# Attention on one core: the value products, transposes and sums of a group gathered in one place of TensorE's order

## The chip, the cores and the metric

The kernel runs on one core of a Trainium2 chip. The metric is the device time of one execution in microseconds; the kernel before took 2106.49 us (median of three runs, 2105.7 to 2106.67).

## What is computed

One layer of an encoder on 1024 tokens of 1024 features, all in float32: attention, a layer norm with a scaled residual, a mixture of experts (4 of 32 for each token), and a second layer norm. The change is in the attention alone:

```python
def attention_mixer(x, w_qkv, q_norm, k_norm, w_o):
    q, k, v = jnp.split(x @ w_qkv, ...)        # 16 heads of q, 4 of k and v, 64 features each
    q, k = apply_rope(rms_norm(q, q_norm)), apply_rope(rms_norm(k, k_norm))
    s = jnp.einsum('bqkgd,bskd->bkgqs', q_blk, k) * scale     # blocks of 128 queries
    p = jax.nn.softmax(s, axis=-1)
    o = jnp.einsum('bkgqs,bskd->bqkgd', p, v)
    return o.reshape(bsz, seq, N_Q_HEADS * HEAD_DIM) @ w_o
```

Every head of k and v serves four heads of q.

## The kernel before, in words

The kernel has four stages: the projections to q, k and v with their norms and rotary positions (to about 160 us of the profile), attention (to about 530 us), the output projection with the norm and the routing, and the experts, whose weights are streamed from memory. A float32 product that must be exact is made of parts that were rounded and what the rounding left ("hi" and "lo").

Attention goes over 8 tiles of 128 queries, `i`, and in each over the 4 heads of keys, `g`. One pair is a *group*, `n = 4 i + g`, with four heads of queries; there are `NG = 32` of them. In a group the loop goes over 8 tiles of 128 keys, `k`; one turn of it is called a step here.

- `probs(n, k)` (L439): two matmuls of 512 columns make the scores of one tile of keys (tile `st`, two buffers), with the negated maxima already in them; ScalarE's exponential writes `pt` (L447, twelve buffers). GpSimd adds up `pt` over the tiles of keys into `acc`, and VectorE makes the last addition (L451).
- `scores(n + 2, m, hf)` (L427): the scores of the group after next the other way round, two matmuls into a tile `sc` of 1024 columns (two buffers), and VectorE's maximum over it (`nm`, L437), four of them a group.
- `maxima_a`, `maxima_b` (L143, L149): the maxima in two parts, transposed by TensorE (`tpm`), and spread by VectorE into the operand `q2` (L155), of which ScalarE copies the other half (L152).
- `pv(n, k)` (L454): the value products of two tiles of keys, side by side on the two halves of TensorE's columns, summed in `po` (one buffer). Each of them shows as two records in the trace. `close_a(n)` (L462) adds the two halves (ScalarE's copy `ob`, L469, and VectorE's two additions, L472).
- `scale_a(i)`, `scale_b(i, hf)` (L478, L494): once a tile of queries, the sums of the exponentials over the keys (`su`, 16 matmuls, 32 records), their reciprocals by a chain on VectorE (L486 to L491), and two matmuls `rb` that spread them, with a multiplication of half the outputs behind each (L499). Then the outputs go to memory.
- `stack_q(i + 1, h)` (L158): four transposes of queries of the next tile (`tpq`), which ScalarE and VectorE take apart (L168 to L172). `tpm`, `tpq`, `su` and `rb` share one buffer in PSUM.

What sets the order: the framework's scheduler places each engine's instructions by their order in the program, when their operands are expected, and by what room is free. Where the code opens `manual_schedule` for an engine, that engine's instructions are kept as they are written. Before, TensorE had an order by hand in the first group alone (L534 to L567). In the others the scheduler placed `pv` pair by pair between the scores, near the places where the loop calls it (steps 3, 5 and 7, and step 1 of the next group for the last pair). VectorE, ScalarE and GpSimd are placed by the scheduler in both kernels. Every engine works through its queue in the order that it was given.

Of the kernel before, what the change touches and what calls it, by code (L numbers as in the profile page):

```python
# [42 lines left out]
def trunk_kernel(ctx: ExitStack, tc: tile.TileContext, x, w_qkv, q_norm, k_norm, w_o,  # L43
# [59 lines left out]
    # ones on the rows that meet the maxima  # L103
# [3 lines left out]
    # the heads' high parts again, and below them the maxima, each at its own head  # L107
    q2s = [p_kv.tile([P, 4, P], F32R, name="q2_0")]
    nc.gpsimd.memset(q2s[0][HD:P].bitcast(F32), 0.0)
    # sums of the heads (g, a, j) on rows (g, r, a, j): r = 0 gives its high part and r = 1 its low part  # L110
# [20 lines left out]
    def first_scores(s, ps):  # L131
        # the first four heads' maxima, in halves
        hf, m = divmod(s, 4)
        if s == 0:
            nms[0] = p_xq.tile([P, 4], F32, tag="nm", bufs=3, name="nm0")
            nms["h"] = p_xq.tile([P, 4, 2], F32, name="nmh")
        sc = ps.tile([P, 512], F32, tag="qkv2", name=f"sc0_{s}")
        mm(sc, qs[0][:, m, :], kT_hi[:, 0, hf * 512:(hf + 1) * 512])
        nc.vector.tensor_reduce(nms["h"][:, m, hf:hf + 1], sc, AX.X, ALU.max, negate=True)
        if s == 7:  # L140
            nc.vector.tensor_reduce(nms[0], nms.pop("h"), AX.X, ALU.min)
# [16 lines left out]
    def stack_q(i, h, ps):  # L158
        # eight heads: the upper half of the partitions holds what rounding leaves
        if h == 0:  # L160
            qs[i] = p_xq.tile([P, NH, P], F32R, tag="cols", bufs=2, name=f"qs{i}")
        qv = qs[i][:, 8 * h:8 * h + 8, :].rearrange("p (j a) t -> p j a t", a=2)
        tp = ps.tile([P, 4, P], F32, tag="tp", name=f"tpq{i}_{h}")
        for c in range(4):
            j = 4 * h + c
            nc.tensor.transpose(tp[:, c, :], ql[i][:, j * P:(j + 1) * P], ident)
        odd = p_xq.tile([P, 4, P], F32R, tag="odd", name=f"odd{i}_{h}")
        nc.scalar.copy(qv[0:HD, :, 0, :], tp[0:HD])  # L168
        nc.scalar.copy(odd[HD:P], tp[HD:P])
        nc.vector.tensor_tensor(qv[HD:P, :, 0, :], tp[0:HD], qv[0:HD, :, 0, :].bitcast(F32), ALU.subtract)  # L170
        nc.vector.tensor_tensor(qv[HD:P, :, 1, :], tp[HD:P], odd[HD:P].bitcast(F32), ALU.subtract)
        nc.scalar.copy(qv[0:HD, :, 1, :], odd[HD:P].bitcast(F32))  # L172

# [1 line left out]
    QKV = (NH + 2 * NKV) * HD  # L175
    nqk = NH + NKV
    with tc.tile_pool(name="p1", bufs=1, side="right", reuse_waits="tile") as p1, \
# [68 lines left out]
        # cosines and sines with the norms' weights and the scale in them  # L246
# [123 lines left out]
    # pieces of the experts' weights, in the order in which they are used  # L370
# [12 lines left out]
    def fetch(upto):  # L383
        while nxt[0] < min(upto, len(seq)):
            e, kind, n = seq[nxt[0]]
            # the first table entry is awaited early, so that the first gathers go ahead of what follows
            e2 = max(e, 2)
            if (e > 1 or nxt[0] == 12) and e2 not in ev:
                with tc.issue_after(last[0]):
                    ev[e2] = nc.values_load(eid[0:1, e2:e2 + 1], engines=[mybir.EngineType.SP],  # L390
                                           min_val=0, max_val=NE - 1)
            x_ = ds(ev[e], 1) if e > 1 else slice(e, e + 1)
            w = slot(order[nxt[0] % len(order)], f"w{e}{kind}{n}")
            with ExitStack() as es:
                if last[0] is not None:
                    es.enter_context(tc.issue_after(last[0]))
                if kind == "g":
                    got = nc.sync.dma_start(w, w_gu[x_, n * P:(n + 1) * P, :].rearrange("o p n -> p (o n)"))
                else:
                    got = nc.sync.dma_start(  # L400
                        w.rearrange("p (k n) -> p k n", k=2),
                        w_dn[x_, 2 * n * P:2 * (n + 1) * P, :].rearrange("o (k p) n -> p (o k) n", p=P))
            last[0] = got.ins
            raw[nxt[0]] = w
            nxt[0] += 1

    # rows of four KB that the output projection and then the experts use
# [12 lines left out]
    with tc.tile_pool(name="p2", bufs=1, side="right", reuse_waits="tile") as p2, \  # L420
# [6 lines left out]
        def scores(n, m, hf):  # L427
            # queries on the partitions, for the maxima
            i, g = divmod(n, NKV)
            if hf == 0:  # L430
                sc[n, m] = ps_s.tile([P, T], F32, tag="sc", name=f"sc{n}_{m}")
            sl = slice(hf * 512, (hf + 1) * 512)
            mm(sc[n, m][:, sl], qs[i][:, 4 * g + m, :], kT_hi[:, g, sl])
            if hf == 1:
                if m == 0:
                    nms[n] = p_xq.tile([P, 4], F32, tag="nm", bufs=3, name=f"nm{n}")
                nc.vector.tensor_reduce(nms[n][:, m:m + 1], sc.pop((n, m)), AX.X, ALU.max, negate=True)  # L437

        def probs(n, k):  # L439
            # keys on the partitions: scores less the maxima, then the exponentials  # L440
# [13 lines left out]
        def pv(n, k):  # L454
            # two tiles of keys side by side
            i, g = divmod(n, NKV)
            if k == 0:
                po[n] = ps_o.tile([P, 4 * P], F32, tag="po", name=f"po{n}")
            for b in range(2):
                mm(po[n][b * HD:(b + 1) * HD], vn[:, k + b, g, :], pts[n, k + b], k == 0, k == NT - 2)  # L460
# [17 lines left out]
        def scale_a(i):  # L478
            # one over the sums over the keys
# [36 lines left out]
        # the table of slots: rows without a token point past the tokens  # L516
# [12 lines left out]
        for r in (1, 2):  # L529
            q2s.append(p2.tile([P, 4, P], F32R, name=f"q2_{r}"))  # L530
            nc.gpsimd.memset(q2s[r][HD:P].bitcast(F32), 0.0)
        for n in range(NG + 1):
            i, g = divmod(n, NKV)
            if n == 0:  # L534
                first = ExitStack()
                first.enter_context(tc.manual_schedule(engines={mybir.EngineType.PE}))
            for k in range(NT):
# [9 lines left out]
                if k == (5 if n == 0 else 2) and n + 1 < NG:  # L547
                    maxima_b(n + 1, ps_t)
                if k == 1 and n > 0:
                    pv(n - 1, NT - 2)  # L550
                    close_a(n - 1)
                if g == 0 and n > 0:
                    if k == 4:
                        scale_a(i - 1)
                    elif k in (5, 7):
                        scale_b(i - 1, k // 7)
                if k in (3, 5, 7) and n < NG:
                    pv(n, k - 3)
                if n < NG and i + 1 < NT:
                    if g == 0 and k == 6:  # L560
                        load_q(i + 1)
                    if g in (1, 2) and k == 0:
                        stack_q(i + 1, g - 1, ps_t)
            if n + 2 < NG:
                maxima_a(n + 2)
            if n == 0:
                first.close()  # L567
            if i in (2, 3) and g == 2:
                load_o(i - 2)
            if i == 4 and g == 2:  # L570
                load_xr(0)
    es_kv.close()
    keep = ctx.enter_context(tc.tile_pool(name="keep", bufs=1, side="left", reuse_waits="tile"))

# [24 lines left out]
    # the first expert's place in the sequence is its own  # L599
# [31 lines left out]
    with tc.tile_pool(name="p3o", bufs=1, side="right", reuse_waits="tile") as p3o, \  # L631
# [43 lines left out]
        def norm_b(i):  # L675
# [7 lines left out]
            if i == NT - 1:  # L683
                # the table of the exponential comes while the engine waits
# [23 lines left out]
        def route_a2(i):  # L708
            x1T = x1Tn.pop(i)
            # a quarter of the features in each quarter of the columns  # L710
# [13 lines left out]
        def run(*gens):  # L724
            # in turn, an instruction of each
# [28 lines left out]
        def rows_of_first(i, mk, pp):  # L754
            # the slots of the first expert without a way through the table
# [67 lines left out]
        def f_gates(i):  # L823
            # the gates in two parts, twice over, as rows
# [22 lines left out]
        def f_add(i):  # L847
            # alpha * x1 plus the gated second biases of the experts
# [31 lines left out]
        def split_b(i):  # L880
            # the first biases as three parts of eight bits
# [54 lines left out]
        # rank (by count) of the expert at each position of the sequence  # L936
# [28 lines left out]
        # the last tile's way to the first expert's rows, with other work in its gaps  # L965
        L = NT - 1
        with tc.manual_schedule(engines={mybir.EngineType.DVE, mybir.EngineType.Activation,
# [39 lines left out]
            # experts in the order of their counts (the first two stay where they are)  # L1007
# [37 lines left out]
    with tc.tile_pool(name="moex", bufs=1, side="right", reuse_waits="tile") as mx, \  # L1045
# [7 lines left out]
        def slots(finish):  # L1053
            # slots of every expert: the first 128 rows, and the next 32 four times over (a quarter row each)
# [29 lines left out]
        def list_blocks():  # L1084
            # blocks of rows beyond what the unrolled experts take
# [78 lines left out]
        def turn_a(e, part):  # L1164
            if part == 0:
                # the last one has the room of a next expert's rows
# [43 lines left out]
        def gate_up(e, between):  # L1210
# [33 lines left out]
            if by_cols:  # L1244
                # the end goes column by column, and a half's activation as soon as it is there
# [101 lines left out]
    # the rows and the last norm's weights take slots of the stream  # L1347
# [141 lines left out]
```

## Time and profile before

| What | Value |
|---|---|
| time, median of three runs | 2106.49 us |
| span of the profiled execution | 2106.0 us |
| TensorE busy in the span | 2017.2 us (96%) |
| VectorE | 1631.0 us (77%) |
| ScalarE | 1286.0 us (61%) |
| GpSimd | 547.3 us (26%) |
| mean granted clock of TensorE | 0.984 |
| 500 MB moved, mean | 238 GB/s |

The table gives the busy time of each engine in the span; an engine can be busy while it isn't the one that the others wait for. The durations of matmuls overlap, since they are pipelined, so what one of them takes of TensorE's time is read from the distance of two starts. Where a row says "idle before", an arrow names what the engine waited for.

### The profile page before, as it was taken

How to read it: one execution, taken by the hardware profiler on the slowest of the kernel's cores; microseconds unless marked ns; L12 is line 12 of the kernel's file. 1: busy time of each engine (PE TensorE's matmuls, PEld its weight loads, DVE VectorE, ACT ScalarE, POOL GpSimd, SP SyncE). 2: the span in 40 equal slices, each digit the busy share in tenths (PEclk: the TensorE clock that was granted, in tenths of full speed). 3: DMA queues.
4: the chain of work that ended last, by engine and by line, in shares of the span. 5: the costliest groups of instructions: out<-in, count | busy, mean ns of one | idle time of the engine just before them, and what ended most of it. 6: DMA issues, size and time to landing. Idle time of an engine off the chain costs nothing. (4 is left out here: it accounts for less than half of the span.)

```text
span 2106.0 us, 27647 instructions
## 1 busy us (share of the span) xinstructions
PE 2017.2 (96%) x10091; PEld 1348.4 (64%) x10091; DVE 1631.0 (77%) x1771; ACT 1286.0 (61%) x1548; POOL 547.3 (26%) x382
## 2 busy tenths in 40 slices
PE   8999999999997999999999999999999999999990
PEld 6774444444675666666676776777767767677670
DVE  6658788877888777677787787877878778778786
ACT  5656556655555656566676666766756667667562
POOL 1216666675144201111211211111112111110004
PEclk9999999999998999999999999999999999999995
DMA  4116000000646777888888897998989988889765
GB/s 171 70 61 176 31 31 31 28 13 11 231 150 222 292 282 274 295 281 294 325 345 315 325 345 287 350 331 313 351 301 323 352 294 343 331 307 354 274 218 172
DMA packets 106348, 500.36 MB, mean 238 GB/s; under 512 B 16001, under 2 KB 17026, under 8 KB 73442
## 3 DMA queue, kind: packets, MB, share of 16 engines
q1 hardware_dynamic: 86928, 445.45, 55.5%
q0 software_dynamic: 16432, 52.47, 9.4%
q8 instruction: 80, 1.31, 0.2%
q10 hardware_dynamic: 2850, 0.66, 0.2%
q14 instruction: 58, 0.48, 0.1%
HBM read 457.05 MB, written 41.49 MB: 237 GB/s over the span
## 5 line engine op out<-in xcount | busy, mean ns | idle before, releaser
L52 PE MATMUL gu<-wh,xTh 128*128 128x512 f32 x1024 | 419.2, 410 | 1.0 <-ACT xTh L60 1.0
L52 PE MATMUL gu<-wh,xTl 128*128 128x512 f32 x1024 | 407.1, 398 | 0.0
L52 PE MATMUL gu<-wl,xTh 128*128 128x512 f32 x1024 | 401.3, 393 | 0.2 <-DVE wl L620 0.2
L1304 POOL DMA_INDIRECT fd<-y,mi x32 | 78.8, 2461 | 703.5 <-ACT y L1303 700.4
L447 ACT ACTIVATE pt<-st 128x512 f32<-128x512 f32 x256 | 150.7, 598 | 134.4 <-PE st L52 102.8
L52 PEld LDWEIGHTS gu<-wh,xTh 128*128 128x128 f32 x1024 | 192.8, 188 | 54.0 <-ACT wh L615 11.7
L52 PEld LDWEIGHTS gu<-wl,xTh 128*128 128x128 f32 x1024 | 192.8, 188 | 42.1 <-DVE wl L620 0.8
L52 PEld LDWEIGHTS gu<-wh,xTl 128*128 128x128 f32 x1024 | 193.2, 189 | 38.5 <-issue 3.6
L451 POOL TENSOR_TENSOR acc<-acc,pt 128x512 f32<-128x512 f32 x152 | 201.5, 1326 | 48.6 <-ACT pt L447 38.8
L52 PE MATMUL yp<-wh,aTh 128*128 128x512 f32 x512 | 204.1, 399 | 0.0
L52 PE MATMUL yp<-wl,aTh 128*128 128x512 f32 x512 | 202.2, 395 | 0.0
L52 PE MATMUL yp<-wh,aTl 128*128 128x512 f32 x512 | 200.6, 392 | 0.0
L437 DVE TENSOR_REDUCE nm<-sc 128x1 f32<-128x1024 f32 x124 | 150.5, 1221 | 28.8 <-PE sc L52 27.9
L52 PE MATMUL po<-pt,vn 128*64 128x512 f32 x512 | 135.6, 615 | 2.1 <-DVE ot L472 2.1
L606 POOL DMA_INDIRECT xg<-xd,mi x32 | 54.6, 1708 | 314.5 <-PE tpx L1145 306.3
L52 PEld LDWEIGHTS yp<-wh,aTh 128*128 128x128 f32 x512 | 96.0, 188 | 49.1 <-ACT wh L615 29.3
L52 PE MATMUL qkv<-wh,xT 128*128 128x512 f32 x384 | 123.5, 402 | 2.6 <-ACT xT L60 1.4
L52 PE MATMUL st<-qs,kT_hi 128*128 128x512 f32 x256 | 116.5, 455 | 3.4 <-ACT pt L447 3.3
L52 PEld LDWEIGHTS st<-qs,kT_hi 128*128 128x128 f32 x256 | 47.9, 187 | 97.7 <-ACT pt L447 66.7
L52 PEld LDWEIGHTS yp<-wl,aTh 128*128 128x128 f32 x512 | 96.3, 188 | 21.3 <-DVE wl L620 0.8
L52 PEld LDWEIGHTS yp<-wh,aTl 128*128 128x128 f32 x512 | 96.1, 188 | 19.2
L52 PE MATMUL st<-q,kT_lo 128*128 128x512 f32 x256 | 102.3, 400 | 0.6 <-DVE q L155 0.6
(515 smaller groups left out, 4180.0 us busy)
## 6 DMA issues: line engine op xcount, KB each, us to landing
w0g<-in_expert_w_gate_up SPq DMA_DIRECT2D x8, 1024.0 KB, 7.2
w1g<-in_expert_w_gate_up SPq DMA_DIRECT2D x8, 1024.0 KB, 7.2
w2g<-in_expert_w_gate_up SPq DMA_DIRECT2D x8, 1024.0 KB, 8.6
w3g<-in_expert_w_gate_up SPq DMA_DIRECT2D x8, 1024.0 KB, 6.8
w4g<-in_expert_w_gate_up SPq DMA_DIRECT2D x8, 1024.0 KB, 7.2
w5g<-in_expert_w_gate_up SPq DMA_DIRECT2D x8, 1024.0 KB, 6.4
w6g<-in_expert_w_gate_up SPq DMA_DIRECT2D x8, 1024.0 KB, 6.8
w7g<-in_expert_w_gate_up SPq DMA_DIRECT2D x8, 1024.0 KB, 7.1
```

Source lines behind the costliest of these rows:

```text
L52: nc.tensor.matmul(o, lhsT=lhsT, rhs=rhs, start=start, stop=stop)
L437: nc.vector.tensor_reduce(nms[n][:, m:m + 1], sc.pop((n, m)), AX.X, ALU.max, negate=True)
L447: nc.scalar.activation(pts[n, k], st, AF.Exp)
L451: (nc.vector if k == 7 or n == NG - 1 or n == NG - 2 and k > 3 else nc.gpsimd).tensor_tensor(accs[n], pts[n, 0] if k == 1 else accs[n], pt ...
L606: return nc.gpsimd.indirect_dma_start(out=xg[e], out_offset=None, in_=xd, in_offset=bass.IndirectOffsetOnAxis(ap=mi[:, e:e + 1] if rows is ...
L1304: nc.gpsimd.indirect_dma_start(out=fd, out_offset=bass.IndirectOffsetOnAxis(ap=mi[:, e:e + 1], axis=0), in_=y, in_offset=None, bounds_chec ...
```

## The change

The value products of a whole group are now made together, in step 3 of the next group, behind that step's scores. With them stand the sums of the tile before (first group of a tile; before the value products) or four transposes of the next tile's queries (second and third group), and, behind them, the transpose of the next group's maxima. TensorE's order by hand now covers all groups. `scale_b` stays at steps 5 and 7, and the load of queries at step 6, of the first group of a tile. Comments were taken out elsewhere.

```diff
-        def pv(n, k):
+        def pv(n):
             i, g = divmod(n, NKV)
-            if k == 0:
-                po[n] = ps_o.tile([P, 4 * P], F32, tag="po", name=f"po{n}")
-            for b in range(2):
-                mm(po[n][b * HD:(b + 1) * HD], vn[:, k + b, g, :], pts[n, k + b], k == 0, k == NT - 2)
+            po[n] = ps_o.tile([P, 4 * P], F32, tag="po", name=f"po{n}")
+            for k in range(0, NT, 2):
+                for b in range(2):
+                    mm(po[n][b * HD:(b + 1) * HD], vn[:, k + b, g, :], pts[n, k + b], k == 0, k == NT - 2)
...
+        pe_order = ExitStack()
+        pe_order.enter_context(tc.manual_schedule(engines={mybir.EngineType.PE}))
         for n in range(NG + 1):
             i, g = divmod(n, NKV)
-            if n == 0:
-                first = ExitStack()
-                first.enter_context(tc.manual_schedule(engines={mybir.EngineType.PE}))
             for k in range(NT):
...
-                if k == (5 if n == 0 else 2) and n + 1 < NG:
+                if n < NG and i + 1 < NT and g == 0 and k == 6:
+                    load_q(i + 1)
+                if k == 3 and n > 0:
+                    if g == 0 and n < NG:
+                        scale_a(i - 1)
+                    elif g in (1, 2) and i + 1 < NT:
+                        stack_q(i + 1, g - 1, ps_t)
+                    pv(n - 1)
+                    close_a(n - 1)
+                    if n == NG:
+                        scale_a(i - 1)
+                if k == (5 if n == 0 else 3) and n + 1 < NG:
                     maxima_b(n + 1, ps_t)
-                if k == 1 and n > 0:
-                    pv(n - 1, NT - 2)
-                    close_a(n - 1)
-                if g == 0 and n > 0:
-                    if k == 4:
-                        scale_a(i - 1)
-                    elif k in (5, 7):
-                        scale_b(i - 1, k // 7)
-                if k in (3, 5, 7) and n < NG:
-                    pv(n, k - 3)
-                if n < NG and i + 1 < NT:
-                    if g == 0 and k == 6:
-                        load_q(i + 1)
-                    if g in (1, 2) and k == 0:
-                        stack_q(i + 1, g - 1, ps_t)
+                if g == 0 and n > 0 and k in (5, 7):
+                    scale_b(i - 1, k // 7)
             if n + 2 < NG:
                 maxima_a(n + 2)
-            if n == 0:
-                first.close()
...
+        pe_order.close()
```

## Rows read from the trace of the kernel before

**Rows 1.** The view of stretches: the two moments (us from the start of the span) and the time between them, then the busy time of TensorE, its weight loads, VectorE, ScalarE and GpSimd, each with the number of instructions, then TensorE's granted clock, the busy share of the DMA engines and GB/s. First all of attention, then one tile of queries.

```profile
160.00:535.00 375.00, 363.89 (x1650) 176.83 (x1650) 296.53 (x413) 222.72 (x385) 245.27 (x190) 1.00 0.15 46
...
331.45:377.31 45.86, 44.90 (x207) 21.95 (x206) 36.73 (x51) 26.97 (x46) 31.70 (x25) 1.00 0.07 24
```

**Rows 2.** The timeline of TensorE: start, length (us), engine, line, what it writes and reads, how many records. One pair of value products between scores, and two pairs in one burst.

```profile
302.48 0.39 PE L52 MATMUL st<-q,kT_lo 128*128 128x512 f32 x1
302.71 0.40 PE L52 MATMUL sc<-kT_hi,qs 128*128 128x512 f32 x1
303.03 1.08 PE L52 MATMUL po<-pt,vn 128*64 128x512 f32 x4
304.04 0.50 PE L52 MATMUL st<-qs,kT_hi 128*128 128x512 f32 x1
304.38 0.40 PE L52 MATMUL st<-q,kT_lo 128*128 128x512 f32 x1
...
503.96 0.40 PE L52 MATMUL sc<-kT_hi,qs 128*128 128x512 f32 x1
504.29 1.94 PE L52 MATMUL po<-pt,vn 128*64 128x512 f32 x8
506.15 0.50 PE L52 MATMUL st<-qs,kT_hi 128*128 128x512 f32 x1
506.49 0.39 PE L52 MATMUL st<-q,kT_lo 128*128 128x512 f32 x1
```

**Rows 3.** The same timeline, the tile of queries from 331.45 to 377.31: the first and the last of its fifteen bursts of value products (the first of eight records, the other fourteen of four), between the two transposes that bound it.

```profile
331.45 0.27 PE L154 MATMUL tpm<-ident,nm 128*8 128x128 f32 x1
332.36 1.94 PE L52 MATMUL po<-pt,vn 128*64 128x512 f32 x8
...
373.61 1.08 PE L52 MATMUL po<-pt,vn 128*64 128x512 f32 x4
377.31 0.27 PE L154 MATMUL tpm<-ident,nm 128*8 128x128 f32 x1
```

**Rows 4.** Groups of TensorE's instructions by line and form in that tile of queries: count, busy us, mean ns of one, idle time before them.

```profile
L52 PE MATMUL po<-pt,vn 128*64 128x512 f32 x64 | 17.0, 616 | 0.3 <-DVE ot L472 0.3
```

**Rows 5.** TensorE's timeline around the sums of one tile alone, around the last sums, which follow value products, and around four transposes of queries.

```profile
307.31 0.40 PE L52 MATMUL sc<-kT_hi,qs 128*128 128x512 f32 x1
307.63 1.08 PE L52 MATMUL su<-acc,which 128*32 128x128 f32 x32
308.64 0.50 PE L52 MATMUL st<-qs,kT_hi 128*128 128x512 f32 x1
...
526.05 1.94 PE L52 MATMUL po<-pt,vn 128*64 128x512 f32 x8
527.93 1.06 PE L52 MATMUL su<-acc,which 128*32 128x128 f32 x26
...
319.16 0.60 PE L166 MATMUL tpq<-ident,ql 128*128 128x128 f32 x4
319.52 0.47 PE L52 MATMUL st<-qs,kT_hi 128*128 128x512 f32 x1
319.83 0.40 PE L52 MATMUL st<-q,kT_lo 128*128 128x512 f32 x1
```

**Rows 6.** TensorE's timeline at two waits on VectorE: a scaling matmul, and a value product.

```profile
315.95 0.50 PE L52 MATMUL st<-qs,kT_hi 128*128 128x512 f32 x1
316.88 0.50 PE L52 MATMUL rb<-rr,half 128*128 128x512 f32 x1 [0.44 <-DVE ot L499]
...
320.57 1.08 PE L52 MATMUL po<-pt,vn 128*64 128x512 f32 x4 [0.35 <-DVE ot L472]
```

**Rows 7.** The timelines of TensorE, ScalarE and the weight loads (PEld) around one reuse of a score buffer.

```profile
225.54 0.39 PE L52 MATMUL st<-q,kT_lo 128*128 128x512 f32 x1
...
226.03 1.23 ACT L447 ACTIVATE pt<-st 128x512 f32<-128x512 f32 x2 [1.01 <-PE st L52]
...
226.68 0.19 PEld L52 LDWEIGHTS st<-qs,kT_hi 128*128 128x128 f32 x1 [0.26 <-ACT pt L447]
...
226.69 0.48 PE L52 MATMUL st<-qs,kT_hi 128*128 128x512 f32 x1
227.01 0.40 PE L52 MATMUL st<-q,kT_lo 128*128 128x512 f32 x1
```

**Rows 8.** Groups of ScalarE's instructions by line and form in the tile of queries of rows 1.

```profile
L447 ACT ACTIVATE pt<-st 128x512 f32<-128x512 f32 x32 | 18.8, 598 | 16.9 <-PE st L52 11.7 <-POOL acc L451 4.1
L152 ACT CAST q<-qs 64x512 fp32r<-64x512 f32 x4 | 2.4, 612 | 0.1
L469 ACT COPY ob<-po 64x512 f32<-64x512 f32 x4 | 2.3, 584 | 1.9 <-PE po L52 1.8
```

**Rows 9.** The same for GpSimd's additions.

```profile
L451 POOL TENSOR_TENSOR acc<-acc,pt 128x512 f32<-128x512 f32 x21 | 27.9, 1327 | 7.3 <-ACT pt L447 6.2
```

**Rows 10.** The same for VectorE.

```profile
L437 DVE TENSOR_REDUCE nm<-sc 128x1 f32<-128x1024 f32 x16 | 19.5, 1222 | 3.9 <-PE sc L52 3.7
L472 DVE TENSOR_TENSOR ot<-po,ob 64x256 f32<-64x256 f32 x9 | 3.7, 416 | 0.9 <-ACT ob L469 0.8
L451 DVE TENSOR_TENSOR acc<-acc,pt 128x512 f32<-128x512 f32 x4 | 2.8, 693 | 2.6 <-POOL acc L451 1.8 <-ACT q L152 0.7
L155 DVE TENSOR_TENSOR q<-tpm,mask 8x512 fp32r<-8x512 f32 x4 | 2.7, 676 | 0.2 <-PE tpm L154 0.2
...
L499 DVE TENSOR_TENSOR ot<-ot,rb 128x512 f32<-128x512 f32 x2 | 1.4, 676 | 0.0
L491 DVE TENSOR_TENSOR rr<-rs,col 128x1024 fp32r<-128x1024 f32 x1 | 1.2, 1224 | 0.0
L486 DVE RECIPROCAL rs<-su 128x128 f32<-128x128 f32 x1 | 1.0, 958 | 1.3 <-PE su L52 1.3
L488 DVE CAST rh<-rs 128x128 fp32r<-128x128 f32 x1 | 0.8, 785 | 0.0
...
L489 DVE SCALAR_TENSOR_TENSOR rs<-rh,low,rs 128x128 f32<-128x128 f32 x1 | 0.4, 352 | 0.0
```

**Rows 11.** The end of attention: the stretch of the last two groups in the view of stretches, and TensorE's timeline where the output projection begins (`hp`).

```profile
508.74:528.92 20.18, 20.01 (x103) 8.33 (x102) 11.42 (x21) 10.96 (x20) 4.24 (x5) 1.00 0.08 24
...
528.92 3.70 PE L52 MATMUL hp<-wo,o 128*128 128x512 f32 x8
532.57 0.47 PE L52 MATMUL rb<-rr,half 128*128 128x512 f32 x1
```

## The prediction

> **What bounds the kernel now.** I read the table by stretches first [rows 1]. Attention (160 to 535 us) holds the whole change: TensorE is busy 363.89 of 375 us at a granted clock of 1.00, VectorE 296.53, GpSimd 245.27, ScalarE 222.72. One period of the pattern, a tile of queries or four groups, lasts 45.86 us from one transpose of the maxima (331.45) to the same one a tile later (377.31); there TensorE is busy 44.90, VectorE 36.73, GpSimd 31.70, ScalarE 26.97. So TensorE sets the time here, with VectorE next at 80%. Two things are to be seen. First, what a TensorE instruction costs the queue is the distance between starts, not its duration, since durations overlap. Second, VectorE's spare 9 us a period are what a shorter period eats.
>
> The profiled span is 2106.0 us, half a microsecond under the median of 2106.49; the sum is made on the span, and 0.5 is added at the end. A difference under 0.2% (4.2 us) counts as none.
>
> **The change part by part.**
>
> *Value products side by side.* A pair of value products (two key tiles, four records) between score matmuls is read start to start [rows 2]: score to pair 0.32 us, pair to next score 1.01, that score to the next 0.34, where plain scores follow at 0.23. So a pair on its own costs 0.32 + 1.01 + 0.34 - 2 x 0.23 = 1.21 us. Two pairs together: 0.33 + 1.86 + 0.34 - 0.46 = 2.07. The second pair costs 0.86, so each joining saves 0.35. In one tile of queries [rows 3] stand fourteen bursts of one pair and one of two, 16 pairs in 15 bursts (first and last shown; 64 records [rows 4]). Afterwards there are four bursts: 11 fewer, 11 x 0.35 = 3.85 us a tile.
>
> *Sums and transposes in the block.* The sum block alone [rows 5] is entered at 0.32 and takes 1.01 like a pair; left like one too (0.34), it costs 1.21. Behind a value block it starts 1.88 after that block, the same 1.86 to 1.88 with which a score starts, so the switch between the two is paid and only about 0.20 goes. The four query transposes cost 0.36 + 0.31 - 0.23 = 0.44; if the exit goes, 0.08 each, 0.16 for two. Together 0.36 a tile; bounds 0 and 0.6. The Trainium skill (TensorEngine Tiling (Array Packing), Key Properties) says that changing the tiling mode drains TensorE while changing only the tile does not. By that rule joining unlike shapes (32, 64 and 128 columns) keeps the drain and only the pairs gain; without it the sum block would cost 0.86 as a second pair does, 0.15 more gain on each of seven tiles, 1 us. The row of 1.88 agrees with the rule.
>
> *Waits that go.* Once a tile a pair waits for VectorE to empty the one accumulator [rows 6]: 0.74 from the score instead of 0.32, 0.42 lost. After the change the previous block is a whole group back, so this goes: 0.42. Gains together 3.85 + 0.36 + 0.42 = 4.63 a tile.
>
> *Eight score steps without a gap.* Between blocks now come eight steps (4 to 7, then 0 to 3) of two probability scores and one for the maxima, 3 x 0.23 = 0.69 each. The probability scores have two buffers, and ScalarE's exponential frees them. The loop [rows 7]: second score starts 225.54, exponential 226.03 to 226.63, weights of the score that reuses the buffer at 226.68, that score at 226.69 and its partner 0.32 later, not 0.23. That is 1.15 + 0.32 = 1.47 for two steps, 0.735 a step against 0.69. Six of the eight steps can feel it, but the first after each block starts with both buffers free: I take 0.2 us a group, 0.8 a tile; bounds 0 and 6 x 0.10 x 4 = 2.4. Before, a pair stood in nearly every second step and covered this.
>
> *ScalarE's other work.* The copy of the queries (0.61) and the copy out of the accumulator (0.58) [rows 8] now compete with this tight loop. During a block (0.32 + 1.01 + 3 x 0.86 = 3.9 us) ScalarE has no scores, so there is room; the accumulator's copy comes when the block ends, while the first score of step 4 still needs about 0.7 us. I take 0.3 a tile; if the query copy falls between exponentials each time, 4 x 0.6 = 2.4.
>
> *Order by hand: the sum block's wait.* The sums stand first in the block of a tile's first group, so everything on TensorE behind them waits for the last addition of the group before. GpSimd does six additions a group at 1.33 us [rows 9], the seventh is VectorE's 0.69 [rows 10]. Counted from the end of the previous block, by the distances of [rows 7]: exponential 4 ends near 1.45, additions 4 to 6 take until 5.5, VectorE's until 6.2, or 7.2 if a reduction of 1.22 goes before it. TensorE arrives after eight steps, at 5.7 to 6.0. Wait 0.8 on average; bounds 0 and 3.3 (two reductions and the nm cast ahead). One time a tile. Once a tile the maxima's scores also find VectorE late: 0.3 (0 to 1).
>
> *Reciprocal and scaling.* After the sums VectorE does 0.96 + 0.79 + 0.35 + 1.22 = 3.3 us [rows 10], beside 3.6 us of value products: hidden. The second scaling matmul waits for the first's multiplication now as before [rows 6]: 0.93 instead of 0.34, 0.6 lost, and it follows at the same distance of two steps. I change nothing; bounds -0.6 and +1.
>
> *Queues elsewhere.* The loads of queries and of the first outputs move by less than a group on SP, whose queues carry 24 GB/s in this period; no DMA is added. The probability buffers (12) now hold eight of one group and four of the next until the block; step 4 of a group comes behind that block on TensorE anyway. Cost 0.
>
> *Sum.* Net a tile 4.63 - 0.8 - 0.3 - 0.8 - 0.3 = 2.43 us. It holds for groups 1 to 29, 7.25 tiles: 17.6 us. In group 0 the three pairs leave, but VectorE's eight reductions (8 x 1.22 = 9.8) then fill it: nothing. The last two groups have no maxima scores [rows 11], so their steps of 2 x 0.23 fall behind the loop of 0.735: 16 x 0.735 + 3 blocks x 3.8 + sums 1.0 + last exponential 1.1 = 25.3 us, against 20.2 in the row plus three pairs moved in (3.6), 23.8: 1.5 lost. If the scaling of the last tile must finish before the output projection, which now starts at 528.92 with the scaling (532.57) among it, TensorE waits up to 5 us; or not at all: I take 1.5. Span 2106.0 - 17.6 + 3.0 = 2091.4, with 0.5: 2092 us.
>
> **The rivals.**
>
> *The copies dry out the loop (slower).* ScalarE stands still through every block and must then do eight exponentials in about 5.5 us; if in each group the accumulator's copy and the query copy are queued ahead of waiting exponentials, 1.19 us goes a group. It decides from the margin of the other terms: (4.63 - 0.8 - 0.8 - 0.3) / 4 = 0.68 us a group. Loss (1.19 - 0.68) x 29 + 3 = 18: 2124. For: ScalarE works its queue in the order it was given, and the loop has no slack. Against: ScalarE is busy 59% in the period, and the query copy's data are there long before, so it can stand within a block.
>
> *VectorE becomes the bound (no change).* VectorE's 36.73 a tile do not shrink; in a tile's first group they are 4 x 1.22 + 0.69 + 0.84 + 0.68 + 0.6 + 3.3 + 1.36 = 12.4 against TensorE's 5.5 + 0.5 + 3.8 + 1.0 = 10.8. If the sums wait 3.3 instead of 0.8, 2.5 x 7 = 17 goes: 2109, within a point of no change. For: VectorE already waits for GpSimd's sums (1.8 of its 2.6 us at that line [rows 10]). Against: the reductions have two buffers of slack. The Trainium skill (TensorEngine Tiling (Array Packing), PSUM Bottleneck) states just this: tiling speeds TensorE but not the emptying of PSUM, which may become the limit. Here the period would have to fall to 36.73 before that held on average; only the first group of four is over.
>
> *The new waits are hidden.* Without the loop's, copies' and sums' terms except 0.8: 3.83 x 7.25 - 1.5 = 26: 2080.
>
> *That the change doesn't do what it says*: the joining saves only if the eight products really follow each other; nothing in the block needs another engine between them, so I give it no more than the no-change rival holds.
>
> **How the numbers follow.** Forecast 0.45 (2084 to 2102), waits hidden 0.22 (2068 to 2084), VectorE bound 0.15 (2102 to 2111), copies 0.18 (2111 and above). Range 2068 to 2112: it leaves out most of the slower rival and gains of over 38 us (6.1 a tile, all waits gone too). Faster by over 0.2%: 0.45 + 0.22 and a part of the third, 0.69; same 0.11; slower 0.20.
>
> **What would show it.** Right: value bursts of 16 records lasting about 3.6 us, 32 of them; the period of four groups near 43.4 us; idle time of scores released by exponentials, and one wait a tile of the sum block on an addition. Wrong: a period above 45 with ScalarE idle through blocks and copies between exponentials; or the 0.86 not holding for the third and fourth pair; or projection starting several us after the last sums.

## The result, and the profile after

The changed kernel took 2123.93 us (median of four runs) beside 2106.58 of the kernel before (now of four runs too); the ratio is 1.0076, with an interval of 1.0064 to 1.0088. It is slower by 0.8%, where 2092 was forecast, and the time lies above the range (2068 to 2112). Each later time stands with its ratio to runs of the kernel before that were taken beside it, whose medians lie between 2107.9 and 2109.3. One execution, of the kernel reported with 2087.11 us, took 3334.28 us at a granted clock of 0.555 instead of 0.983 and is left out of its ratio.

The view of stretches of the kernel after: all of attention, one tile of queries from one transpose of the maxima (304.61) to the same one a tile later (352.54; the stretch ends at 352.60), as in [rows 1], and six microseconds around a fall of the clock, for the last section.

```profile
160.00:545.00 385.00, 343.20 (x1608) 186.07 (x1607) 324.37 (x407) 212.72 (x379) 245.23 (x190) 0.98 0.15 45
...
304.61:352.60 47.99, 42.44 (x210) 23.18 (x208) 41.70 (x50) 26.50 (x46) 31.66 (x24) 1.00 0.07 23
...
390.00:396.00 6.00, 5.83 (x20) 4.17 (x19) 4.40 (x8) 3.98 (x7) 3.99 (x4) 0.76 0.00 0
```

A tile takes 47.9 us instead of 45.86. TensorE is busy 2.5 us less in it, so the joined products do save; but VectorE is busy 41.70 instead of 36.73 us. TensorE's timeline, where attention passes to the output projection, shows how much of the result lies here:

```profile
545.47 1.08 PE L52 MATMUL su<-acc,which 128*32 128x128 f32 x32
546.48 1.98 PE L52 MATMUL hp<-wo,o 128*128 128x512 f32 x4
```

The projection starts at 546.48 instead of 528.92 [rows 11]: 17.6 us, against 17.4 between the medians. Behind it the two profiles differ by 0.6 us. (One microsecond of the 17.6 is there before attention starts: its first transpose stands at 163.95 instead of 162.94.)

The timeline of TensorE in that tile, the places that matter:

```profile
301.02 3.65 PE L52 MATMUL po<-pt,vn 128*64 128x512 f32 x16
304.61 0.27 PE L154 MATMUL tpm<-ident,nm 128*8 128x128 f32 x1
...
310.86 0.42 PE L52 MATMUL su<-acc,which 128*32 128x128 f32 x6
312.35 1.06 PE L52 MATMUL su<-acc,which 128*32 128x128 f32 x26 [1.07 <-DVE acc L451]
313.34 3.65 PE L52 MATMUL po<-pt,vn 128*64 128x512 f32 x16
...
319.46 0.50 PE L52 MATMUL rb<-rr,half 128*128 128x512 f32 x1 [0.88 <-DVE q L155]
...
322.20 0.50 PE L52 MATMUL rb<-rr,half 128*128 128x512 f32 x1 [0.85 <-DVE ot L499]
...
336.80 3.65 PE L52 MATMUL po<-pt,vn 128*64 128x512 f32 x16
342.56 0.27 PE L154 MATMUL tpm<-ident,nm 128*8 128x128 f32 x1 [2.11 <-DVE qs L171]
```

The block of 16 records takes 304.61 - 301.02 = 3.59 us, which is 1.01 + 3 x 0.86 to the hundredth. All the longer waits are for VectorE. Three of its waits that were not there before, over the whole of attention (us in total, how many, the longest):

```profile
PE tpm L154 <- DVE qs L171: 15.7, 11, 2.1
PE rb L52 <- DVE q L155: 5.4, 7, 0.9
PE su L52 <- DVE acc L451: 2.7, 3, 1.1
```

Who holds VectorE is seen in its own timeline from the end of the second group's block on:

```profile
331.89 2.51 DVE L437 TENSOR_REDUCE nm<-sc 128x1 f32<-128x1024 f32 x2
335.62 1.76 DVE L451 TENSOR_TENSOR acc<-acc,pt 128x512 f32<-128x512 f32 x1 [1.22 <-POOL acc L451]
337.30 1.23 DVE L146 CAST nm<-nm 128x4 fp32r<-128x4 f32 x1
338.45 1.21 DVE L437 TENSOR_REDUCE nm<-sc 128x1 f32<-128x1024 f32 x1
339.58 0.29 DVE L147 TENSOR_TENSOR nm<-nm,nm 128x4 fp32r<-128x4 f32 x1
339.80 1.21 DVE L437 TENSOR_REDUCE nm<-sc 128x1 f32<-128x1024 f32 x1
341.02 0.68 DVE L170 TENSOR_TENSOR qs<-tpq,qs 64x512 fp32r<-64x512 f32 x1
341.72 0.69 DVE L171 TENSOR_TENSOR qs<-tpq,odd 64x512 fp32r<-64x512 f32 x1
```

Read from the bottom: TensorE's transpose at 342.56 waits for L171. L171 stands behind two reductions whose scores were there from about 334.6 and 336.4 on; these stand behind a cast of 1.23 us and an addition of 1.76, and the addition had waited 1.22 us for GpSimd. In VectorE's table for the tile the same two lines stick out: the addition of L451 at 1489 ns instead of 693 [rows 10], with 4.4 us of waits instead of 2.6, and the cast of four columns at 1184 instead of 166. The first two lines are of the kernel after, the third is the cast in the kernel before, in the tile of [rows 10].

```profile
L451 DVE TENSOR_TENSOR acc<-acc,pt 128x512 f32<-128x512 f32 x4 | 6.0, 1489 | 4.4 <-POOL acc L451 4.4
L146 DVE CAST nm<-nm 128x4 fp32r<-128x4 f32 x4 | 4.7, 1184 | 0.0
...
L146 DVE CAST nm<-nm 128x4 fp32r<-128x4 f32 x4 | 0.7, 166 | 0.0
```

In the kernel before, the reductions themselves had 3.9 us of waits for scores in a tile [rows 10]; after it, nearly all the idle time stands at the addition and behind the transposes (L155, 3.5 us). VectorE has become what TensorE waits for.

### The profile page after: what moved, and what is told of

The parts are those of the page before. It is cut to its first block, busy times and chain, and to the rows that moved or that the text cites. A ratio compares the mean times of both kernels' runs of the same rounds, so it can differ in the third digit from the quotient of the medians.

```text
span 2124.2 us, 27573 instructions
## 1 busy us (share of the span) xinstructions
PE 2002.1 (94%) x10059; PEld 1363.2 (64%) x10091; DVE 1663.0 (78%) x1771; ACT 1282.5 (60%) x1548; POOL 548.9 (26%) x382
## 5 line engine op out<-in xcount | busy, mean ns | idle before, releaser
L451 POOL TENSOR_TENSOR acc<-acc,pt 128x512 f32<-128x512 f32 x152 | 199.6, 1313 | 101.2 <-ACT pt L447 91.6
L52 PE MATMUL po<-pt,vn 128*64 128x512 f32 x512 | 117.7, 602 | 0.0
L52 PE MATMUL sc<-kT_hi,qs 128*128 128x512 f32 x256 | 104.0, 411 | 3.2 <-DVE nm L437 3.0
```

What stands on the lines that cost most here:

```text
L52: nc.tensor.matmul(o, lhsT=lhsT, rhs=rhs, start=start, stop=stop)
L451: (nc.vector if k == 7 or n == NG - 1 or n == NG - 2 and k > 3 else nc.gpsimd).tensor_tensor(accs[n], pts[n, 0] if k == 1 else accs[n], pt ...
```

## The experiments

Theory A: VectorE's seventh addition of each group stands in its queue behind GpSimd's late sixth, and what is queued behind it comes late. Theory B: the rival on record at 2124, ScalarE's copies among the exponentials. Theory C: the order by hand itself.

**The addition off VectorE.** One line of the changed kernel gives the seventh addition to GpSimd:

```diff
-  (nc.vector if k == 7 or n == NG - 1 or n == NG - 2 and k > 3 else nc.gpsimd).tensor_tensor(
+  (nc.vector if n >= NG - 2 and (k == 7 or n == NG - 1 or k > 3) else nc.gpsimd).tensor_tensor(
```

> The changed kernel with one edit: the seventh addition of each group's exponentials stands on GpSimd instead of VectorE (the last two groups as they were). Theory A (VectorE's queue stands behind GpSimd's last additions: it waits 4.4 us a tile for them, its own addition takes 1.49 instead of 0.69 us, and reductions, query halves and with them TensorE's transposes come late): that wait and that addition leave VectorE, some 10 us a tile, so 2095 to 2110, less what the sums wait for GpSimd. Theory B (the copies on ScalarE dry out the exponentials, the recorded rival of 2124): nothing changes for ScalarE, 2119 to 2128.

2091.63 us (two runs; ratio 0.9917, 0.9888 to 0.9946), 3 us below the range of theory A and far from that of B. The tile in the view of stretches, TensorE's longest wait in it, and the cast of the maxima on VectorE:

```profile
302.54:346.10 43.56, 42.09 (x208) 23.08 (x206) 38.26 (x47) 26.57 (x46) 35.72 (x28) 1.00 0.07 25
...
306.74 0.50 PE L52 MATMUL rb<-rr,half 128*128 128x512 f32 x1 [0.84 <-DVE ot L499]
...
L146 DVE CAST nm<-nm 128x4 fp32r<-128x4 f32 x4 | 4.8, 1192 | 0.1
```

43.6 us a tile, where the forecast had 43.4, and no transpose waits for L171 any more, though GpSimd now does more work (35.72 us of 43.56). ScalarE's instructions in the tile stand in the same order as before the edit. This speaks for A against B. The cast still takes 1.19 us, so its length alone doesn't make VectorE late. Run again for an interval:

> The first run's kernel once more, for an interval: 2089 to 2096 beside 2105 to 2109 of the kernel before.

2092.94 us (0.9926, 0.9909 to 0.9942).

**GpSimd's additions left out.** Tiles 2 to 6 are not added, and the first addition is of a constant:

```diff
-            else:
+            elif k == 1:
+                nc.gpsimd.tensor_scalar(accs[n], pts[n, 1], 1.0, None, ALU.add)
+            elif k == 7:
```

> The changed kernel, with GpSimd's additions of tiles 2 to 6 left out and the first replaced by the exponentials plus a constant, so the sums are not those of the reference. Theory A: VectorE neither waits for GpSimd nor shares its access to memory with it; its addition falls to 0.7 us and the cast of the maxima from 1.18 to 0.17 us, the period of four groups from 48.0 to 42 to 44 us: 2085 to 2102. Theory B: ScalarE's queue is as before, 2117 to 2128.

2149.8 us, outside both ranges, and no measure of attention: from the projection's start on it takes 68 us longer than the changed kernel, and 470 MB are read from memory instead of 457. That the other sums send the tokens to other experts is the likely reason; no run shows it. Attention alone can be read. One tile lasts 42.13 us (transposes at 300.06 and 342.19), the projection starts at 505.0 instead of 546.5. VectorE's seventh addition is still there, without waits and at its old length:

```profile
L453 DVE TENSOR_TENSOR acc<-acc,pt 128x512 f32<-128x512 f32 x4 | 2.7, 684 | 0.1
```

So it is not that addition as such, but its waiting for GpSimd and its standing beside GpSimd's additions; the edit ends both. The casts of the maxima in the same stretch (L146) take 0.16 and 0.17 us again.

**Old places, order by hand.** The kernel before with `manual_schedule` around all groups, the four pairs left where the loop calls them.

> The kernel before, with TensorE's order by hand in all groups but the value products left in four pairs where the loop calls them, no block. Theory C (it is the order by hand, not the block, that costs): 2118 or more. Theories A and B (it is the block, which lets exponentials and with them GpSimd's additions come in one burst): within 6 us of before, 2101 to 2113.

2165.07 us (1.0265, 1.0235 to 1.0295): in theory C's range, and larger than any theory had it. (Whether C holds for the changed kernel, the next run asks.) The places written in the loop are bad ones when they are kept. Its waits from 164 to 560 us (attention lasts until 586):

```profile
PE rb L52 <- DVE rr L491: 26.2, 7, 3.7
PE tpm L154 <- DVE qs L171: 13.9, 14, 2.0
```

The scaling matmuls follow the sums by one step and wait up to 3.7 us for the reciprocals, which the scheduler had covered and the block covers. The granted clock in attention is 0.95 instead of 1.00, which is a part of the loss too. So the scheduler's freedom was worth 56 us to the four pairs; with TensorE's order by hand, the block gives 41 of them back (2123.93).

**The block without the order by hand.**

```diff
         for n in range(NG + 1):
+            if n == 1:
+                pe_order.close()
...
-        pe_order.close()
```

> The changed kernel, block and all, but with TensorE's order left to the scheduler from the second group on. It cuts the first value product off the block in some groups (one more switch, 0.35 us). If the order by hand is what costs, 2100 or less; if the block's effect on VectorE and GpSimd is, the same as the changed kernel within 6 us, 2116 to 2130.

2132.85 us (two runs; 1.0115, 1.0087 to 1.0143), somewhat above the expected range. With the block, the order by hand costs nothing; theory C falls for the changed kernel.

**The block turned round.** The maxima's transpose first, then the products, then the query transposes or the sums.

```diff
-                    if g == 0 and n < NG:
+                    if n + 1 < NG:
+                        maxima_b(n + 1, ps_t)
+                    pv(n - 1)
+                    close_a(n - 1)
+                    if g == 0:
                         scale_a(i - 1)
                     elif g in (1, 2) and i + 1 < NT:
                         stack_q(i + 1, g - 1, ps_t)
-                    pv(n - 1)
-                    close_a(n - 1)
-                    if n == NG:
-                        scale_a(i - 1)
-                if k == (5 if n == 0 else 3) and n + 1 < NG:
+                if n == 0 and k == 5:
                     maxima_b(n + 1, ps_t)
```

> The changed kernel with the block turned round: the transpose of the maxima first, then the value products, then the transposes of queries or the sums. Theory A: the transpose of the maxima no longer waits for VectorE's query halves (15.7 us in 11 waits) and TensorE's clock does not fall after the long ones (three falls inside, some 1.7 us each); the scaling matmuls, two steps behind the sums, wait longer, up to 2 us a tile. 2104 to 2114. Theory B: 2119 to 2128.

2242.92 us (1.0634, 1.0603 to 1.0665): a miss of 130 us, mostly by two waits that I had made myself (below from 164 to 560 us; attention lasts until 666).

```profile
PE tpm L154 <- DVE nm L147: 55.2, 26, 3.9
PE rb L52 <- DVE rr L491: 24.3, 6, 4.1
```

The transpose now leads the block and waits for the second part of the maxima, which stood far back in the same delayed queue; and the scaling matmuls come two steps after the sums without the products between. The granted clock from 160 to 545 us is 0.90, which adds to the loss. The run tells nothing between A and B; in the changed kernel the 3.6 us of products in the middle hid most of both chains.

**The addition by itself in the kernel before.** The same line.

> The kernel before, with the seventh addition of each group on GpSimd and nothing else. If the block is what gains once VectorE is free of that addition, this alone changes little, since TensorE is the bound there and VectorE has 9 us a tile to spare: 2103 to 2109. If the addition was a burden in the kernel before too, it falls by itself to 2090 to 2098 and the block has no part in the 2091.6 of the first run.

2114.64 us (1.0030, 1.0020 to 1.0040): a little slower, above the expected range. So the 2092 is not the gain of moving the addition by itself; it needs the block.

**The addition's place in the queue.** It stays on VectorE, but behind the second reduction of the next group (`add` makes the addition as before, `reds[0]` is the last reduction issued):

```diff
+                if k == 3 and 0 < n < NG - 1:
+                    with tc.issue_after(reds[0]):
+                        add(n - 1, 7)
```

> The changed kernel; the seventh addition stays on VectorE but is queued behind the second reduction of the next group, at the block. If it is the place in the queue (reductions, query halves and transposes stood behind an addition that was not ready), the wait of 4.4 us a tile goes, the addition lies in the block's time, and the sums wait some 1.5 us longer once a tile: 2100 to 2112. If it is the work (the addition itself, lengthened to 1.49 us beside GpSimd), little is gained: 2116 to 2125.

2106.21 us (0.9995, 0.9984 to 1.0006), in the range given for the place. The move is worth 17.7 of the 32 us between the changed kernel and the first run. The waits of attention show most of the rest; the second line is the addition on VectorE from 200 to 490 us:

```profile
PE su L52 <- DVE acc L455: 15.2, 7, 2.4
...
L455 DVE TENSOR_TENSOR acc<-acc,pt 128x512 f32<-128x512 f32 x26 | 22.0, 847 | 0.0
```

The sums wait for the late addition once in each of seven tiles, 15.2 us (in the first run 2.5, for GpSimd); the transposes wait for the query halves no more. But the move also takes the addition out of its wait and, mostly, out of GpSimd's way: it takes 0.85 us on average, where it took 1.22 in the changed kernel (200 to 510 us). So what the place is worth and what the length is worth stay unseparated in this run as in the others.

**ScalarE's copy in the block.** `maxima_b` holds the copy (L152) behind the exponential of step 3 (`exps[0]`, the last one issued), in the changed kernel and in that of the first run.

```diff
-        nc.scalar.copy(q2[0:HD], qs[i][0:HD, 4 * g:4 * g + 4, :].bitcast(F32))
+        with ExitStack() as es:
+            if n > 1:
+                es.enter_context(tc.issue_after(exps[0]))
+            nc.scalar.copy(q2[0:HD], qs[i][0:HD, 4 * g:4 * g + 4, :].bitcast(F32))
```

> The changed kernel with the same edit to ScalarE's copy alone; the seventh addition stays on VectorE. The recorded rival (copies among the exponentials cost about 1.2 us a group, 2124 in all) gives 2105 or less. Theory A (VectorE's queue behind GpSimd) gives 2118 to 2126, since VectorE's order is not touched.

2124.24 us (1.0072, 1.0055 to 1.0088), the same as the changed kernel. Theory B falls: the copies cost nothing there, while VectorE is late. That its time on record, 2124, is the measured one is chance.

> The first run's kernel (seventh addition on GpSimd) with ScalarE's copy of the queries held behind the exponential of step 3, so that it lies in the block. In that run eight steps took about 6.0 us where they cost TensorE 5.5. If the copy between exponentials is what stretches them, some 0.3 us a group goes over 29 groups: 2080 to 2087. If the loop over the two score buffers does it without the copy, or the query halves come late behind the copy, 2089 to 2095.

2087.11 us (0.9898, 0.9878 to 0.9918), 5.8 below the 2092.94 beside it: once VectorE is out of the way, the copy does cost 0.2 us a group. With the copy held in both kernels, taking the addition off VectorE is worth 37 us (2124.24 and 2087.11, side by side). This is the fastest version found, and it beats the kernel before by 1.0%.

**Scaling two steps later**, in the first run's kernel: at step 7 of the first group and step 1 of the second.

> The first run's kernel (seventh addition on GpSimd) with the two scaling matmuls two steps later, at step 7 of a tile's first group and step 1 of the second. Their waits for VectorE (7.2 us on the matmul queue in that run, and the exposed weight loads behind them) go: 2081 to 2088, against 2091.6. If those waits only stand in for others behind them, 2089 to 2093.

2094.54 us (0.9937, 0.9915 to 0.9959), no gain, and a little above the range. The wait of 0.84 is replaced by two of 0.53 and 0.41, the second at the query transposes:

```profile
308.19 0.49 PE L52 MATMUL rb<-rr,half 128*128 128x512 f32 x1 [0.53 <-DVE ot L499]
...
310.49 0.66 PE L166 MATMUL tpq<-ident,ql 128*128 128x128 f32 x4 [0.41 <-DVE ot L499]
```

These operations share one buffer in PSUM, and each waits until what the one before left there has been read.

## Why the prediction was wrong, point by point

- *Joining the products*: right to the hundredth (3.59 us a block). The switch to the sums stays, as the row of 1.88 had it: sums to products takes 0.99 (312.35 to 313.34). This agrees with the rule of the Trainium skill (TensorEngine Tiling (Array Packing), Key Properties) that changing the tiling mode drains TensorE. The query transposes take 0.53 to the products (325.50 to 326.03 in the timeline), not the 0.36 that I had counted with their exit saved: 0.17 more, twice a tile.
- *The accumulator's wait*: gone, as forecast.
- *The sum block's wait*: this step failed. I worked out that GpSimd's sixth addition comes 5.5 us after a block (in the tile shown it ends 5.9 after, at 310.51), and then priced it "one time a tile", at the sums. But the seventh addition stands in VectorE's queue in every group, ahead of a cast, two reductions and, in two groups of a tile, the query halves, for which TensorE's next transpose waits. At the sums the wait is only 2.7 us in all of attention; at the transposes it is 15.7 and at the first scaling matmuls 5.4, neither of which had a term. The price was not 0.8 us a tile: the edit that takes it away is worth 32 us, 4.4 us a tile over 7.25 tiles.
- *Its size*: I took 0.69 us for the addition from a row in which it met no addition of GpSimd, and the cast of the maxima (0.17 before) had no term for meeting one. In the tile shown they take 1.49 and 1.18, 4 x (0.80 + 1.02) = 7.3 us of VectorE's time (from 200 to 510 us the means are 1.22 and 1.03). VectorE's wait for GpSimd grew less: 26.6 us in attention (27 times) from 17.1 (19 times). The cast stayed as long when the addition was gone and the time fell to 2092, so it is not the cast that decides; between the addition's wait and its length no run decides. [Rows 10] could have warned: the cast of the reciprocals (L488) took 0.79 there, beside an addition of GpSimd (356.10 to 357.38), and 0.23 at 530.55, where none ran.
- *Eight steps without a gap*: mis-sized. In the kernel of 2087.11 us, without a copy among them, a stretch runs from 311.73 to 317.68 (transpose to transpose), 5.95 us where 8 x 0.69 are 5.52. Of the 0.43 more, 0.12 stand behind the transpose, as they did in the kernel before (331.45, 331.48, 331.80); the loop costs 0.3 a group, not 0.2. The copy adds 0.2, not 0.08.
- *Reciprocal and scaling*: the reciprocals are hidden by the products, as forecast; but both scaling matmuls wait, 0.88 and 0.85. The first wait is new: it is for `q2` (L155), which stands behind the delayed work and must empty the shared buffer. In the first run, where VectorE isn't late, it is gone.
- *The end of attention*: the projection starts 1.01 us after the last sums begin and the scaling stands among it, so the 1.5 us that I had put there were not needed.
- *The rivals*: "VectorE becomes the bound" named the engine but stopped at 2109, because it too counted the delay only at the sums. "The copies dry out the loop" had the time and the wrong mechanism.
- *Smaller slips*: I added 0.5 us from span to time, where the kernel after shows 1.9 (2124.2 and 2126.1); and 38 us over 7.25 tiles are 5.2 a tile, not 6.1. Neither moves the result.
- *TensorE's clock*: it had no term. It fell four times in attention, which is worth some 6 us (last section).

With the seventh addition off VectorE, 2091.6 and 2092.9 were measured against the 2092 of the forecast. That supports the gain from the joined products, but the closeness is partly luck: the loop, the copies and the query transposes cost more than their terms, and the sums (a wait of 0.35 instead of 0.8) and the end of attention cost less.

## What to carry to other kernels

When work is moved into a burst on one engine, follow each of its consumers' chains to its end and look at which queue the end stands in: an operation that waits can delay all that is queued behind it, in every turn of the loop, not only where its own result is needed. An engine with 20% to spare on average can become the bound when its work must lie between two bursts. And a duration taken from the old profile holds only while the engines that meet there still meet as seldom.

## What the runs showed of the hardware

Some instructions of VectorE took longer beside GpSimd's additions. VectorE's 128 x 512 addition took up to 1.76 us there and the cast of 128 x 4 took 1.23; with GpSimd's additions left out they took 0.68 and 0.16 to 0.17. One tile of the kernel after shows both cases:

```profile
318.50 4.05 POOL L451 TENSOR_TENSOR acc<-acc,pt 128x512 f32<-128x512 f32 x3 [3.72 <-ACT pt L447]
324.63 1.29 POOL L451 TENSOR_TENSOR acc<-pt,pt 128x512 f32<-128x512 f32 x1 [2.09 <-ACT pt L447]
...
322.58 0.69 DVE L451 TENSOR_TENSOR acc<-acc,pt 128x512 f32<-128x512 f32 x1 [0.44 <-POOL acc L451]
...
324.92 1.03 DVE L146 CAST nm<-nm 128x4 fp32r<-128x4 f32 x1
```

The addition at 322.58 lies between GpSimd's additions and takes 0.69; the cast at 324.92 starts beside one and ends with it, at 325.95 and 325.92. GpSimd's own pairs of additions take 2.94 to 2.95 us with VectorE's addition and cast beside them (336.91, 349.47) and 2.61 to 2.63 without (301.31, 326.01). The Trainium skill (GPSIMD Engine Reference, Key points) says that GpSimd shares its interfaces to SBUF with VectorE and contends with its instructions in a two-port mode or with two inputs in SBUF; the rows agree for the addition (two inputs in SBUF), and that the cast runs in such a mode is not shown by a row.

TensorE's clock fell behind some of the waits. The timeline after a wait of 2.07 us for L171:

```profile
389.10 0.27 PE L154 MATMUL tpm<-ident,nm 128*8 128x128 f32 x1 [2.07 <-DVE qs L171]
...
391.11 0.63 PE L52 MATMUL sc<-kT_hi,qs 128*128 128x512 f32 x1
391.54 0.63 PE L52 MATMUL st<-qs,kT_hi 128*128 128x512 f32 x1
391.97 0.63 PE L52 MATMUL st<-q,kT_lo 128*128 128x512 f32 x1
```

Starts are 0.43 us apart instead of 0.23, the engine's level of 1.2 instead of 2.4 GHz, until 392.8; the granted clock of the six microseconds is 0.76. Eight such distances cost 8 x 0.2 = 1.6 us. The same happened behind the waits of 2.10 us at 293.17 and 484.75, and once in the second group (181 to 187 us), behind a wait of 1.79 for the maxima: four falls, some 6 us by this estimate. Behind the wait of 2.11 us at 342.56 it did not fall, so the length of the wait alone does not say it. In the kernel before it was 1.00 in all of attention [rows 1].
